# Merging two branches of a decoder layer: transfers issued by ScalarE at fixed units instead of by SP

## The chip, the cores and the metric

The kernel runs on one core of one Trainium2 chip. The metric is the device time of one execution in microseconds (us). Before the change three runs took 2646.43, 2651.6 and 2653.45 us; the median is 2651.6. Profiles are taken by the hardware on one further execution each.

The engines are TensorE (PE, matrix products), VectorE (DVE), ScalarE (ACT), GpSimd (POOL) and SyncE (SP). Each has its own in-order instruction stream. A transfer (DMA) is started by an instruction in the stream of one of them; an instruction that has to wait for a semaphore holds up everything behind it in its stream, transfers included.

## The reference

One hybrid decoder layer in float32, batch 1, sequence 1024, width 1024: half a SwiGLU FFN, a token mixer with two branches on one normalised input, half a second SwiGLU FFN, a final RMSNorm. Branch A is a gated DeltaNet; branch B attention over the top 256 causal keys per query, chosen by an indexer. Cut to the part in question:

```python
o_sa = dsa_attention(cq, ckv, k_idx, w_idx, w_uq, w_uk, w_uv, w_iq, rel_bias)   # branch B
o_dn = rmsnorm(o_dn, dn_out_norm) * silu(dn_z)                                 # branch A
merged = sigmoid(gate_a) * o_dn + sigmoid(gate_b) * o_sa
x = x + merged @ w_o
# inside dsa_attention, per block of 128 queries and head (8 heads of 128):
p = softmax(where(valid, q_lat @ c_sel * 128**-0.5 + bias, -inf))
o = (p @ c_sel) @ w_uv
```

## The kernel before, in words

Products keep float32 accuracy by splitting each operand into a high part and a remainder. `split` (L109) casts the high part on ScalarE (L111) and subtracts on VectorE or POOL (L112); `mm3` (L137) then issues three matmuls, high·high (L139), high·remainder (L140) and remainder·high (L141).

The stage in question is the attention (`attn_head`, L1295), some 1600 to 1900 us into the execution. All is laid out transposed: 128 channels of a head on the partitions, 1024 positions along the row. The heads 0 to 7 follow each other. A head has four units g in the order 0, 1, 3, 2; unit g holds the query blocks 2g and 2g+1, against all keys up to them, so units 3 and 2 are the long ones. In a unit

- TensorE makes the logits `pl`; VectorE adds bias and mask and keeps the row maximum (`a_mx`, L1322); ScalarE takes the exponential with the row's sum (`a_sum`, L1327);
- TensorE transposes the probabilities into `pp` (L1335); ScalarE casts `ph` (L1338), VectorE subtracts `plo` (L1339); TensorE accumulates `pao` = probabilities times values;
- ScalarE copies `pao` to `osa` (L1344). This copy ends the unit.

Work for later heads runs between: `attn_qk` (queries and keys of the next head: products `pqk`, ScalarE's p at L1288, VectorE's p at L1289), asked for after unit 1 with a priority that lets it move forward, and `attn_values` once per pair of heads, before the even one (products `pav`, then `vh` L1271 and `vl` L1272). Their weights w_uq, w_uk and w_uv come by SP into a rotating buffer `w_raw` (`attn_weights`, L1253) and are split on ScalarE and POOL into `wa`.

The merge (L1359) is done twice per head, for the first 512 positions (h = 0) after unit 1 and for the others (h = 1) after unit 2. Branch A (`odd`), its gate (`zgd`) and tanh of half the gate of branch B (`gbd`) lie in DRAM; a half of a head of each is 128 x 512, 256 KB. The softmax's denominators stand one per partition (128 x 4) and are wanted along the row: `a_rd` writes 0.5 / sum as 512 single numbers to DRAM (L1378), and `a_rb` reads them back to all partitions (L1380). SP issues `od`, `zg`, `gb` (L1369), `a_rd` and `a_rb` in a row, each with one buffer but `a_rd`. One or two units later `done` (L1382) runs: POOL `od` *= `zg` (L1383), VectorE `osa` *= `a_rb` (L1384) and `osa` = (`gb` + 1) `osa` (L1385), POOL `mr` = `od` + `osa` (L1386). The last half uses TensorE to spread the denominators instead of `a_rd` and `a_rb`.

The order of each engine's instructions is set when the program is built, by a scheduler that simulates the engines with priorities; `issue_after` keeps an instruction behind another one in it, and `high_priority` moves one forward. So an edit moves instructions of other parts too.

Of the kernel before, what the change touches and what calls it, by code (L numbers as in the profile page):

```python
# [20 lines left out]
P = 128  # L21
# [49 lines left out]
class Layer:  # L71
# [1188 lines left out]
    def attn_values(self, pair, p, ps):  # L1260
        nc = self.nc
        wh, wl = self.attn_weights(self.I["w_uv"][0][:, 2 * pair:2 * pair + 2, :].rearrange("r h d -> r (h d)"), 256, p, "wuv")
        vh = p.tile([P, NT, 256], F32R, name="vh", tag="vh", bufs=1)
        vl = p.tile([P, NT, 256], F32R, name="vl", tag="vl", bufs=1)
        for t in range(0, NT, 2):
# [5 lines left out]
            nc.scalar.copy(vh[:, t:t + 2, :], pv)  # L1271
            nc.vector.tensor_sub(vl[:, t:t + 2, :], pv, vh[:, t:t + 2, :])  # L1272
# [22 lines left out]
    def attn_head(self, hd, p, ps, qk, values, merged, ahead):  # L1295
# [6 lines left out]
        osa = p.tile([P, S], F32, name="osa", tag="osa", bufs=2)  # L1302
        for g in (0, 1, 3, 2):
            probs = []
# [25 lines left out]
            for j in range(0, 2 * g + 2, 2):  # L1330
# [9 lines left out]
                for i in range(2):  # L1340
                    a, b = (0, 256) if i == 0 else (256, n)
                    out = po[:, 0:256] if b - a == 256 else po[:, 128:256]
                    self.mm3(out, vh[:, j + i, hv], vl[:, j + i, hv], ph[:, a:b], pl_[:, a:b], j + i == 0, j + i == 2 * g + 1)
            nc.scalar.copy(osa[:, ts(g, 256)], po[:, 0:256])  # L1344
            if g == 1:
                ahead()
            for late in self.outs:
                late[0] -= 1
            while self.outs and self.outs[0][0] == 0:
                with self.tc.issue_after(dve.ins):  # L1350
                    self.outs.pop(0)[1]()
            if g in (1, 2):
                out = self.merge(hd, g // 2, sums, osa, p, ps, merged)
                if hd == H - 1 and g == 2:
                    out()
                else:
                    self.outs.append([g, out])

    def merge(self, hd, h, sums, osa, p, ps, merged):  # L1359
# [6 lines left out]
        od, zg, gb = (p.tile([P, 512], F32, name=n, tag=n, bufs=1) for n in ("od", "zg", "gb"))  # L1366
        v = ts(h, 512)
        for x, src in ((od, self.odd[hd][:, v]), (zg, self.zgd[hd][:, v]), (gb, self.gbd[hd][:, v])):
            nc.sync.dma_start(x, src)  # L1369
        if hd == H - 1 and h == 1:  # L1370
# [5 lines left out]
        else:  # L1376
            rd = self.dram.tile([512], F32, name="a_rd", tag="a_rd", bufs=2)
            nc.sync.dma_start(rd.rearrange("(t i) -> i t", i=P), r)  # L1378
            rb = p.tile([P, 512], F32, name="a_rb", tag="a_rb", bufs=1)
            nc.sync.dma_start(rb, rd.partition_broadcast(P))  # L1380

        def done():  # L1382
# [302 lines left out]
```

## Time and profile before

| | |
|---|---|
| median of three runs | 2651.6 us |
| the profiled execution | 2654.08 us |
| its span on the profile | 2652.1 us |
| mean granted TensorE clock | 0.971 |
| busy: TensorE, VectorE, ScalarE, POOL | 2519.1, 1737.9, 1198.3, 970.9 us |

The span is what the trace covers; the execution's own time is 2.0 us longer. Busy times are sums over the span. The granted clock is a share of TensorE's full 2.4 GHz; in a stretch at 0.5 the engine ran at 1.2 GHz. Waits are listed by the instruction that waits and the one it waited for.

### The profile page before, as it was taken

To read this page: it belongs to the slowest core of one execution; us is meant where nothing else is said; L and a number is where in the kernel's file an instruction comes from. 1 tells how busy PE (TensorE), PEld (TensorE's weight loads), DVE (VectorE), ACT (ScalarE), POOL (GpSimd) and SP (SyncE) were. 2 spreads that over 40 slices of the span, in tenths; PEclk is the share of its full clock that TensorE was granted. 3 is DMA by queue.
4 is the path that set the end of the run, shared out by engine and by line. 5 is a ranking of instruction groups with operands and counts; after the bars stand their busy time and mean duration, and the time that the engine had idled before them with its cause. 6 is when DMAs were issued, how large, how long until landed. Compare 5 with 4: busy or idle time off the path is not lost.

```text
span 2652.1 us, 36132 instructions
## 1 busy us (share of the span) xinstructions
PE 2519.1 (95%) x12526; PEld 2054.9 (77%) x12526; DVE 1737.9 (66%) x3424; ACT 1198.3 (45%) x2338; POOL 970.9 (37%) x748
## 2 busy tenths in 40 slices
PE   6999999999999899989999999779898999999998
PEld 5788888888787688777778778678776888888886
DVE  7655555676555677999566866566668555546676
ACT  6444344333434665544368446445434434434333
POOL 5555444343434233332100002333446545543340
PEclk8999999999999899999999999889998999999999
DMA  5443346753444155445633323333632344347642
GB/s 168 136 143 129 113 146 219 255 194 101 120 114 122 41 140 139 115 124 123 200 124 116 124 82 74 82 76 78 200 111 94 102 143 143 127 150 263 224 151 75
DMA packets 375607, 356.67 MB, mean 134 GB/s; under 512 B 95417, under 2 KB 279553, under 8 KB 374401
## 3 DMA queue, kind: packets, MB, share of 16 engines
q1 hardware_dynamic: 371840, 348.60, 42.1%
q10 hardware_dynamic: 2304, 4.20, 0.4%
q0 software_dynamic: 1280, 1.57, 0.3%
q8 instruction: 99, 1.62, 0.3%
q14 instruction: 84, 0.68, 0.1%
HBM read 238.28 MB, written 116.01 MB: 134 GB/s over the span
## 4 chain that ended last, share of the span: by engine, by line
PE 40%; DVE 9%; DMA 6%; issue 2%; ACT 1%; POOL 1%; SPq 0%; DVEq 0%; POOLq 0%; ACTq 0%
PE pst L139 7%; PE pst L141 7%; PE pst L140 7%; PE pin L141 2%; PE pin L139 2%; PE pin L140 2%; DVE sb_p L1034 2%; DMA a_rd<-a_r 2%; DMA od<-odd 1%; PE pn L1221 1%; PE po L1230 1%; PE pv L1216 1%; DVE cv_y L923 1%; PE pq L1211 1%; PE pwo L141 1%
## 5 line engine op out<-in xcount | busy, mean ns | idle before, releaser
L140 PE MATMUL pst<-p,w_hi 128*128 128x512 f32 x992 | 392.1, 395 | 8.6 <-DVE p L112 8.5
L139 PE MATMUL pst<-p,w_hi 128*128 128x512 f32 x992 | 393.2, 397 | 4.1 <-ACT p L111 2.3
L141 PE MATMUL pst<-p,w_hi 128*128 128x512 f32 x992 | 391.3, 395 | 0.5 <-DVE w_hi L112 0.5
L139 PE MATMUL pin<-p,w_hi 128*128 128x512 f32 (+1 forms) x848 | 342.1, 405 | 6.0 <-DVE cv_y L923 4.2
L111 ACT CAST w_hi<-w_raw 128x512 fp32r<-128x512 f32 (+3 forms) x294 | 204.1, 695 | 311.7 <-PE pst L141 135.8
L140 PE MATMUL pin<-p,w_hi 128*128 128x512 f32 (+1 forms) x848 | 340.5, 402 | 0.5 <-DVE p L112 0.5
L141 PE MATMUL pin<-p,w_lo 128*128 128x512 f32 (+1 forms) x848 | 340.8, 402 | 0.0
L112 DVE TENSOR_TENSOR w_lo<-w_raw,w_lo 128x512 fp32r<-128x512 f32 (+1 forms) x196 | 188.3, 963 | 167.2 <-ACT w_lo L111 165.6
L140 PE MATMUL pst<-p,w_lo 128*128 128x512 f32 x744 | 292.7, 394 | 3.7 <-DVE p L112 3.7
L141 PE MATMUL pst<-p,w_lo 128*128 128x512 f32 x744 | 292.2, 393 | 1.2 <-DVE w_lo L112 1.2
L139 PE MATMUL pst<-p,w_lo 128*128 128x512 f32 x744 | 290.6, 396 | 0.5 <-ACT c L360 0.5
L140 PEld LDWEIGHTS pst<-p,w_hi 128*128 128x128 f32 x992 | 188.3, 190 | 53.9 <-DVE p L112 12.9
L139 PEld LDWEIGHTS pst<-p,w_hi 128*128 128x128 f32 x992 | 188.8, 190 | 47.3 <-ACT p L111 3.5
L141 PEld LDWEIGHTS pst<-p,w_hi 128*128 128x128 f32 x992 | 188.5, 190 | 43.0 <-DVE w_hi L112 1.3
L111 ACT CAST w_lo<-w_raw 128x512 fp32r<-128x512 f32 (+1 forms) x200 | 115.7, 582 | 207.4 <-PE pst L141 97.8
L139 PEld LDWEIGHTS pin<-p,w_hi 128*128 128x128 f32 (+1 forms) x848 | 161.6, 191 | 42.7 <-DVE cv_y L923 4.5
L141 PEld LDWEIGHTS pin<-p,w_lo 128*128 128x128 f32 (+1 forms) x848 | 161.5, 190 | 37.7 <-issue 3.8
L140 PEld LDWEIGHTS pin<-p,w_hi 128*128 128x128 f32 (+1 forms) x848 | 161.6, 191 | 37.5 <-issue 4.0
L373 DVE TENSOR_TENSOR c<-c,pst 128x512 f32<-128x512 f32 x132 | 89.9, 682 | 150.9 <-PE pst L141 118.1
L112 POOL TENSOR_TENSOR w_lo<-w_raw,w_hi 128x1024 fp32r<-128x1024 f32 (+1 forms) x43 | 107.0, 2488 | 199.4 <-ACT w_hi L111 189.4
L140 PEld LDWEIGHTS pst<-p,w_lo 128*128 128x128 f32 x744 | 140.7, 189 | 35.1 <-DVE p L112 4.9
L141 PEld LDWEIGHTS pst<-p,w_lo 128*128 128x128 f32 x744 | 140.7, 189 | 33.5 <-DVE w_lo L112 2.1
(427 smaller groups left out, 5393.8 us busy)
## 6 DMA issues: line engine op xcount, KB each, us to landing
p<-mixd SPq DMA_DIRECT2D x144, 256.0 KB, 5.4
w_raw<-in_w_in_dram SPq DMA_DIRECT2D x52, 512.0 KB, 4.1
w_raw<-in_ffn_wg_dram SPq DMA_DIRECT2D x44, 512.0 KB, 3.6
w_raw<-in_ffn_wu_dram SPq DMA_DIRECT2D x44, 512.0 KB, 4.0
mixd<-t_hi SPq DMA_DIRECT2D x72, 256.0 KB, 4.3
mixd<-t SPq DMA_DIRECT2D x72, 256.0 KB, 3.8
w_raw<-in_ffn_wd_dram SPq DMA_DIRECT2D x48, 384.0 KB, 4.1
actd<-c SPq DMA_DIRECT2D x70, 256.0 KB, 2.0
```

The costliest lines, as they stand in the source:

```text
L111: self.nc.scalar.copy(hi, raw)
L112: self.pin((self.nc.vector if engine == "vector" else self.nc.gpsimd).tensor_sub(lo, raw, hi))
L139: mm(ps, lhsT=wh, rhs=rh, start=first, stop=False, **kw)
L140: mm(ps, lhsT=wh, rhs=rl, start=False, stop=False, **kw)
L141: mm(ps, lhsT=wl, rhs=rh, start=False, stop=last, **kw)
L373: nc.vector.tensor_add(c[i, h], c[i, h], bank["y" if m == 1 else "z"])
L923: nc.vector.scalar_tensor_tensor(y[:, n:512], pps[h][:, 0:512 - n], cw[:, j:j + 1], y[:, n:512], ALU.mult, ALU.add)
L1034: nc.vector.tensor_mul(v, T[:, 0:i, 0:i].rearrange("p j c -> p c j"), L[:, None, 0:i, i].to_broadcast([P, i, i]))
L1211: nc.tensor.matmul(pq[:, i, :], lhsT=kq[:, h, ts(c, P)], rhs=old[:, h, :], start=True, stop=True)
L1216: nc.tensor.matmul(pv[r, i, :], lhsT=X[r, h, :], rhs=vb[r, h, :], start=True, stop=True)
L1221: nc.tensor.matmul(pn[:, i, :], lhsT=kd[r, h, :], rhs=vn[r, h, :], start=True, stop=True)
L1230: nc.tensor.matmul(po[r, i, :], lhsT=at[r, h, :], rhs=vn[r, h, :], start=True, stop=True)
```

## The change

All transfers of the merge are issued by ScalarE, right behind the copy that ends a unit: after unit 1 the `a_rb` and `gb` of the previous head's second half, this head's first `a_rd`, and the second half of `zg`; after unit 3 the `a_rb` and `gb` of the first half; after unit 2 the second `a_rd`, and for the next head `odd` and the first half of `zg`. `odd` is loaded for a whole head at once (128 x 1024) into the tile `mr` in which the merged head ends up, and multiplied there by POOL (`other_branch`, L1389 of the changed kernel) in units 0 and 3; `od` is gone. The products with `a_rb` and `gb` on VectorE follow one unit after `a_rb`. `merge` and `other_branch` are generators that advance from unit to unit. `osa` becomes three tiles of 512 columns, `zg` keeps one buffer, `a_rb` and `gb` get two. `vh` and `vl` become four tiles each, of two key blocks. Lines of the changed kernel: `a_rd` L1376, `a_rb` L1381, `gb` L1383, `odd` L1392, `zg` L1396, POOL's product L1398, its sum L1387.

SP's queue in front of the weights of the third pair of heads (`w_uv`; `w_uq` and `w_uk` are those of queries and keys, `near` a bias tile), before:
```order
L1369 DMA zg<-zgd 128x512
L1380 DMA a_rb<-a_rd 128x512
L1369 DMA gb<-gbd 128x512
L1369 DMA od<-odd 128x512
L1378 DMA a_rd<-a_r 128x4x1
L1369 DMA zg<-zgd 128x512
L1256 DMA w_raw<-in_w_uv_dram 128x2x256
L1380 DMA a_rb<-a_rd 128x512
L1369 DMA gb<-gbd 128x512
L1256 DMA w_raw<-in_w_uq_dram 128x2x128
```

and now, in front of the same pair's w_uv (the last row but one):
```order
L1256 DMA w_raw<-in_w_uk_dram 128x2x128
L584 DMA near<-nb_wide 128x256
L1256 DMA w_raw<-in_w_uv_dram 128x2x256
L1256 DMA w_raw<-in_w_uq_dram 128x2x128
L1256 DMA w_raw<-in_w_uk_dram 128x2x128
L1256 DMA w_raw<-in_w_uq_dram 128x2x128
L584 DMA near<-nb_wide 128x256
L1256 DMA w_raw<-in_w_uk_dram 128x2x128
L584 DMA near<-nb_wide 128x256
L1256 DMA w_raw<-in_w_uv_dram 128x2x256
L1256 DMA w_raw<-in_w_uq_dram 128x2x128
```

Before, the load of w_uv stands behind four loads of the merge, an `a_rd` and an `a_rb`. Now SP holds weights and `near` only.

ScalarE from the copy that ends unit 1 of head 1 to the one that ends unit 3, before:
```order
L1344 COPY osa<-pao 128x256
L1327 ACTIVATE w_hi,a_sum<-w_hi,a_nm 128x640
L1338 CAST ph<-pp 128x512
L1327 ACTIVATE w_lo,a_sum<-w_lo,a_nm 128x768
L1327 ACTIVATE w_hi,a_sum<-w_hi,a_nm 128x128
L1327 ACTIVATE w_lo,a_sum<-w_lo,a_nm 128x256
L1338 CAST ph<-pp 128x384
L1327 ACTIVATE w_hi,a_sum<-w_hi,a_nm 128x384
L1338 CAST ph<-pp 128x512
L1327 ACTIVATE w_lo,a_sum<-w_lo,a_nm 128x512
L1344 COPY osa<-pao 128x256
```

and now (the last rows follow the copy of unit 3):
```order
L1344 COPY osa<-pao 128x256
L1381 DMA a_rb<-a_rd 128x512
L1383 DMA gb<-gbd 128x512
L1376 DMA a_rd<-a_r 128x4x1
L1396 DMA zg<-zgd 128x512
L1338 CAST ph<-pp 128x512
L1338 CAST ph<-pp 128x384
L1338 CAST ph<-pp 128x512
L1344 COPY osa<-pao 128x256
L1381 DMA a_rb<-a_rd 128x512
```

Before, casts and exponentials alone stand between the copies. Now four transfers stand there, the first of them (`a_rb`) needing a landed `a_rd`, and behind the copy of unit 3 comes an `a_rb` that needs the `a_rd` issued behind the copy of unit 1. The exponentials of the next head's first units have moved ahead of the first copy.

POOL within head 2 (`mr_14141` is head 2's merged tile; `wa` of 256 columns in both halves belongs to w_uq or w_uk, of 512 to w_uv; `nb` a bias), before:
```order
L112 TENSOR_TENSOR wa<-w_raw,wa 128x256
L112 TENSOR_TENSOR wa<-w_raw,wa 128x512
L1386 TENSOR_TENSOR mr_14141<-od,osa 128x512
L112 TENSOR_TENSOR wa<-w_raw,wa 128x256
L1383 TENSOR_TENSOR od<-od,zg 128x512
L1309 TENSOR_TENSOR nb<-near,mask_5848 128x256
```

and now:
```order
L112 TENSOR_TENSOR wa<-w_raw,wa 128x256
L1398 TENSOR_TENSOR mr_14141<-mr_14141,zg 128x512
L112 TENSOR_TENSOR wa<-w_raw,wa 128x256
L112 TENSOR_TENSOR wa<-w_raw,wa 128x512
L1309 TENSOR_TENSOR nb<-near,mask_5848 128x256
L1309 TENSOR_TENSOR nb<-near,mask_5849 128x256
L1309 TENSOR_TENSOR nb<-near,mask_5846 128x256
L112 TENSOR_TENSOR wa<-w_raw,wa 128x256
```

Before, the product `od` *= `zg` follows the splits of `wa` in this stretch; now the product on the merged tile stands between them, in front of the second small one.

```diff
--- before.py
+++ after.py
@@ -1260,16 +1260,15 @@
     def attn_values(self, pair, p, ps):
         nc = self.nc
         wh, wl = self.attn_weights(self.I["w_uv"][0][:, 2 * pair:2 * pair + 2, :].rearrange("r h d -> r (h d)"), 256, p, "wuv")
-        vh = p.tile([P, NT, 256], F32R, name="vh", tag="vh", bufs=1)
-        vl = p.tile([P, NT, 256], F32R, name="vl", tag="vl", bufs=1)
+        vh, vl = ([p.tile([P, 2, 256], F32R, name=n, tag=f"{n}{t}", bufs=1) for t in range(NT // 2)] for n in ("vh", "vl"))
         for t in range(0, NT, 2):
             pv = ps.tile([P, 2, 256], F32, name="pav", tag="qk")
             for i in range(2):
                 for k in range(2):
                     lh, ll = (x[2 + k][t // 4][:, ts((t + i) % 4, P)] for x in self.lat)
                     self.mm3(pv[:, i, :], lh, ll, wh[:, k, :], wl[:, k, :], k == 0, k == 1)
-            nc.scalar.copy(vh[:, t:t + 2, :], pv)
-            nc.vector.tensor_sub(vl[:, t:t + 2, :], pv, vh[:, t:t + 2, :])
+            nc.scalar.copy(vh[t // 2], pv)
+            nc.vector.tensor_sub(vl[t // 2], pv, vh[t // 2])
         return vh, vl
 
     def attn_qk(self, hd, p, ps):
@@ -1292,15 +1291,16 @@
             qk.append((hi, lo))
         return qk
 
-    def attn_head(self, hd, p, ps, qk, values, merged, ahead):
+    def attn_head(self, hd, p, ps, qk, values, merged, ahead, other):
         nc = self.nc
         near = self.near_tile(p, hd)
         (qh, ql), (kh, kl) = qk
         vh, vl = values
         hv = slice((hd % 2) * P, (hd % 2) * P + P)
         sums = self.stat.tile([P, NT], F32, name="a_sum")
-        osa = p.tile([P, S], F32, name="osa", tag="osa", bufs=2)
         for g in (0, 1, 3, 2):
+            if g in (0, 3):
+                osa = p.tile([P, 512], F32, name="osa", tag="osa", bufs=3)
             probs = []
             for b in (2 * g, 2 * g + 1):
                 W = (b + 1) * P
@@ -1340,21 +1340,21 @@
                 for i in range(2):
                     a, b = (0, 256) if i == 0 else (256, n)
                     out = po[:, 0:256] if b - a == 256 else po[:, 128:256]
-                    self.mm3(out, vh[:, j + i, hv], vl[:, j + i, hv], ph[:, a:b], pl_[:, a:b], j + i == 0, j + i == 2 * g + 1)
-            nc.scalar.copy(osa[:, ts(g, 256)], po[:, 0:256])
-            if g == 1:
-                ahead()
-            for late in self.outs:
-                late[0] -= 1
-            while self.outs and self.outs[0][0] == 0:
-                with self.tc.issue_after(dve.ins):
-                    self.outs.pop(0)[1]()
-            if g in (1, 2):
-                out = self.merge(hd, g // 2, sums, osa, p, ps, merged)
-                if hd == H - 1 and g == 2:
-                    out()
-                else:
-                    self.outs.append([g, out])
+                    self.mm3(out, vh[j // 2][:, i, hv], vl[j // 2][:, i, hv], ph[:, a:b], pl_[:, a:b], j + i == 0, j + i == 2 * g + 1)
+            act = nc.scalar.copy(osa[:, ts(g % 2, 256)], po[:, 0:256])
+            ahead(hd, g)
+            with self.tc.issue_after(dve.ins), self.tc.issue_after(act.ins):
+                for out in self.outs:
+                    next(out, None)
+                if g in (1, 2):
+                    out = self.merge(hd, g // 2, sums, osa, p, ps, merged)
+                    next(out)
+                    self.outs = self.outs[-1:] + [out]
+                other(hd, g)
+            if hd == H - 1 and g == 2:
+                for out in self.outs:
+                    for _ in out:
+                        pass
 
     def merge(self, hd, h, sums, osa, p, ps, merged):
 
@@ -1363,11 +1363,9 @@
         r = self.stat.tile([P, 4], F32, name="a_r")
         nc.vector.reciprocal(r, sums[:, ts(h, 4)])
         nc.vector.tensor_scalar_mul(r, r, 0.5)
-        od, zg, gb = (p.tile([P, 512], F32, name=n, tag=n, bufs=1) for n in ("od", "zg", "gb"))
         v = ts(h, 512)
-        for x, src in ((od, self.odd[hd][:, v]), (zg, self.zgd[hd][:, v]), (gb, self.gbd[hd][:, v])):
-            nc.sync.dma_start(x, src)
-        if hd == H - 1 and h == 1:
+        last = hd == H - 1 and h == 1
+        if last:
             rb = ps.tile([P, 512], F32, name="a_rp", tag="pt")
             for t in range(4):
                 d = p.tile([P, P], F32, name="a_d", tag="near", bufs=2)
@@ -1375,17 +1373,30 @@
                 nc.tensor.matmul(rb[:, ts(t, P)], lhsT=self.ones, rhs=d, start=True, stop=True)
         else:
             rd = self.dram.tile([512], F32, name="a_rd", tag="a_rd", bufs=2)
-            nc.sync.dma_start(rd.rearrange("(t i) -> i t", i=P), r)
-            rb = p.tile([P, 512], F32, name="a_rb", tag="a_rb", bufs=1)
-            nc.sync.dma_start(rb, rd.partition_broadcast(P))
-
-        def done():
-            nc.gpsimd.tensor_mul(od, od, zg)
-            nc.vector.tensor_mul(osa[:, v], osa[:, v], rb)
-            nc.vector.scalar_tensor_tensor(osa[:, v], gb, 1.0, osa[:, v], ALU.add, ALU.mult)
-            nc.gpsimd.tensor_add(merged[:, v], od, osa[:, v])
-
-        return done
+            nc.scalar.dma_start(rd.rearrange("(t i) -> i t", i=P), r)
+            yield
+            if h == 1:
+                yield
+            rb = p.tile([P, 512], F32, name="a_rb", tag="a_rb", bufs=2)
+            nc.scalar.dma_start(rb, rd.partition_broadcast(P))
+        gb = p.tile([P, 512], F32, name="gb", tag="gb", bufs=2)
+        nc.scalar.dma_start(gb, self.gbd[hd][:, v])
+        yield
+        nc.vector.tensor_mul(osa, osa, rb)
+        nc.vector.scalar_tensor_tensor(osa, gb, 1.0, osa, ALU.add, ALU.mult)
+        (nc.vector if last else nc.gpsimd).tensor_add(merged[:, v], merged[:, v], osa)
+
+    def other_branch(self, hd, p, merged):
+
+        nc = self.nc
+        nc.scalar.dma_start(merged, self.odd[hd])
+        for h in range(2):
+            v = ts(h, 512)
+            zg = p.tile([P, 512], F32, name="zg", tag="zg", bufs=1)
+            nc.scalar.dma_start(zg, self.zgd[hd][:, v])
+            yield
+            nc.gpsimd.tensor_mul(merged[:, v], merged[:, v], zg)
+            yield
 
 
     def out_proj(self, m, ps, after_tile, after_half):
@@ -1617,15 +1628,23 @@
                 raw = [mlp.tile([P, S], F32, name=f"mr{k}", tag=f"mr{k}") for k in range(NK)]
                 qk = self.qk
 
-                def ahead():
-                    if len(qk) < H:
+                others = [self.other_branch(k, p, raw[k]) for k in range(H)]
+                next(others[0])
+
+                def other(hd, g):
+                    for k, at in ((hd, (0, 1, 3)), (hd + 1, (2,))):
+                        if k < H and g in at:
+                            next(others[k], None)
+
+                def ahead(hd, g):
+                    if hd + 1 < H and g == 1:
                         with self.tc.high_priority(offset=AHEAD):
-                            qk.append(self.attn_qk(len(qk), (p, "wqk", 2), ps))
+                            qk.append(self.attn_qk(hd + 1, (p, "wqk", 2), ps))
 
                 for i in range(H):
                     if i % 2 == 0:
                         vals = self.attn_values(i // 2, p, ps)
-                    self.attn_head(i, p, ps, qk[i], vals, raw[i], ahead)
+                    self.attn_head(i, p, ps, qk[i], vals, raw[i], ahead, other)
                 hs.close()
                 mp = self.pool(ms, "merged", 1, "right")
                 hi, lo = ([mp.tile([P, S], F32R, name=f"{n}{k}", tag=f"{n}{k}") for k in range(NK)] for n in ("mh", "ml"))
```

## Rows read from the trace of the kernel before

**Rows 1.** Three stretches: busy us and count of each engine, PEclk, DMA share, GB/s
```profile
1700.00:1720.00 20.00, 9.11 (x30) 7.13 (x31) 6.03 (x18) 5.02 (x13) 5.72 (x6) 0.57 0.37 90
1720.00:1740.00 20.00, 20.00 (x137) 18.30 (x136) 15.00 (x54) 11.80 (x29) 9.34 (x13) 1.00 0.15 34
1625.50:1894.50 269.00, 224.57 (x1398) 198.56 (x1398) 171.94 (x503) 133.43 (x303) 96.34 (x104) 0.90 0.34 81
```

**Rows 2.** ScalarE's timeline, each head's last copy: start, us, engine, line, [wait]
```profile
1654.09 0.37 ACT L1344 COPY osa<-pao 128x256 f32<-128x256 f32 x1 [0.34 <-PE pao L141]
1681.14 0.39 ACT L1344 COPY osa<-pao 128x256 f32<-128x256 f32 x1
1727.05 0.36 ACT L1344 COPY osa<-pao 128x256 f32<-128x256 f32 x1
1751.23 0.39 ACT L1344 COPY osa<-pao 128x256 f32<-128x256 f32 x1
1797.70 0.36 ACT L1344 COPY osa<-pao 128x256 f32<-128x256 f32 x1
1822.04 0.39 ACT L1344 COPY osa<-pao 128x256 f32<-128x256 f32 x1
```

**Rows 3.** TensorE's waits, 1600 to 1905: us in total, times, longest
```profile
PE pqk L139 <- DVE p L1289: 22.2, 4, 9.1
PE pl L139 <- DVE a_mx L1322: 9.9, 3, 5.1
PE pqk L141 <- POOL wa L112: 1.7, 2, 1.0
```

**Rows 4.** TensorE's timeline, three first products of `pqk`
```profile
1701.77 0.79 PE L139 MATMUL pqk<-p,wa 128*128 128x512 f32 x1 [2.90 <-DVE p L1289]
1715.04 0.79 PE L139 MATMUL pqk<-p,wa 128*128 128x512 f32 x1 [8.15 <-DVE p L1289]
1784.90 0.80 PE L139 MATMUL pqk<-p,wa 128*128 128x512 f32 x1 [9.10 <-DVE p L1289]
```

**Rows 5.** ScalarE's waits, 1600 to 1905
```profile
ACT wa L111 <- DMA w_raw<-in_w_uv_dram: 36.5, 3, 17.7
```

**Rows 6.** Waits in SP's queue, 1600 to 1905
```profile
SPq L1369 <- POOL od L1383: 91.0, 15, 12.5
SPq L1380 <- DMA a_rd<-a_r: 85.2, 12, 11.2
```

**Rows 7.** DMA issues: of 1600 to 1900, and of the page; KB each, us to landing
```profile
a_rd<-a_r SPq DMA_DIRECT2D x15, 2.0 KB, 11.5
actd<-c SPq DMA_DIRECT2D x70, 256.0 KB, 2.0
```

**Rows 8.** Transfers in the chain of waits, 1590 to 1910; last line: SP's timeline
```profile
1683.33 10.89 DMA od<-odd
1703.94 9.19 DMA w_raw<-in_w_uv_dram
1727.77 11.67 DMA a_rd<-a_r
1753.47 10.99 DMA a_rd<-a_r
...
1682.62 0.42 SPq L1378 DMA_DIRECT2D a_rd<-a_r  x1
```

**Rows 9.** VectorE's waits, 1600 to 1905
```profile
DVE osa L1384 <- DMA a_rb<-a_rd: 26.7, 9, 6.3
```

**Rows 10.** ScalarE's timeline, one DMA issue
```profile
1591.04 0.33 ACTq L1125 DMA_DIRECT2D gbd<-tb  x1
```

**Rows 11.** Costliest groups by form, 1590 to 1910: busy, mean ns | idle before
```profile
L1338 ACT CAST ph<-pp 128x512 fp32r<-128x512 f32 x48 | 28.1, 587 | 18.1 <-PE pp L1335 16.2 <-PE pao L141 1.4
L1383 POOL TENSOR_TENSOR od<-od,zg 128x512 f32<-128x512 f32 x16 | 22.3, 1395 | 112.4 <-DMA od<-odd 62.3 <-issue 50.1
L112 POOL TENSOR_TENSOR wa<-w_raw,wa 128x256 fp32r<-128x256 f32 x14 | 10.7, 767 | 28.4 <-ACT wa L111 28.4
```

## The prediction

> **What bounds the kernel now.** I began with busy time by stretch. From the first to the last copy of an attention result (the stage that the change touches) TensorE is busy 224.57 of 269.0 us [rows 1]: 44.4 us are idle, and the granted clock averages 0.90. The reader is to see that no other engine comes near: VectorE has 171.9 and ScalarE 133.4 us of work there. So TensorE's own work sets the end, plus whatever makes it wait.
>
> The losses are uneven. Window 1700 to 1720 has TensorE busy for 9.11 us at a clock of 0.57; the next 20 us are full, 137 matmuls at clock 1.00, so 0.146 us each [rows 1]. The ends of five heads stand at 1681.14, 1727.05, 1751.23, 1797.70 and 1822.04, with head 0's at 1654.09 [rows 2]: head 1 takes 27.05 us, head 2 45.91, head 3 24.18, head 4 46.47, head 5 24.34. The even heads carry `attn_values` besides, but that is not all.
>
> The waits name the rest. TensorE waits 22.2 us in four waits for VectorE's p (L1289) before `pqk`, 1.7 us for POOL's `wa` there, and 9.9 us in three for `a_mx` before `pl` [rows 3]. Two of the four stand in head 2 (2.90 and 8.15) and the longest, 9.10, in head 4 [rows 4]. VectorE is not the cause: behind it ScalarE stands 36.5 us in three waits for the weights w_uv [rows 5]. ScalarE works in order, so the `pqk` results queue behind the cast of w_uv, and VectorE's halves of them with it. And w_uv is late because SP's queue stands in order too: 85.2 us until an `a_rd` has landed (L1380), 91.0 us until POOL has freed `od` (L1369) [rows 6]. `a_rd` is 2 KB in 512 pieces of four bytes, and takes a median of 11.5 us to land [rows 7]; the chain of waits has it at 10.99 and 11.67, an `od` issued right behind one (1682.62, then 1683.33) at 10.89, and w_uv at 9.19 [rows 8].
>
> **The change part by part.** I sum against the profiled execution, 2654.08 us (span 2652.1), 2.5 us above the median of 2651.6.
>
> *Removed: the weight stall.* SP keeps only weights and `near`, so w_uv is issued as soon as its buffer is free. The waits before `pqk` go: 22.2 + 1.7 = 23.9 us [rows 3]. In 1700 to 1720 a mean of 0.57 means 17.2 us at the lower level (1.2 GHz); TensorE was busy for at most 9.1 us of them, and half of that is what the clock cost, some 4.0 a head [rows 1]. Heads 2 and 4 together: 92.38 - 23.9 - 8.0 = 60.5, so 30.2 us each undisturbed. If the clock stays low, 8 us less is gained.
>
> The rows show besides that what follows an `a_rd` into SP's queue is slow: `od` 10.89, w_uv 9.19 us [rows 8]. A rule of the Trainium skill ("DMA: Bandwidth & Descriptors", section "Queues, rings and completion order") speaks against this part of the change: the increment that tells of a landed transfer comes only after all earlier writes of the same DMA engine, whatever queue they came by. By it w_uv from SP would still land with an `a_rd` of ScalarE's, up to some 10 us late; by the rows, which show it within one queue only, w_uv is free of it. I take the gain whole, because w_uv is now issued early enough to bear 10 us, and keep the other as rival C.
>
> *Removed: VectorE's wait for `a_rb`.* 26.7 us in nine [rows 9]; what TensorE sees of it is at most the 9.9 us of `a_mx` [rows 3], and 5.1 of these stand in head 1.
>
> *Added: the same waits on ScalarE.* Some seventy transfers at 0.33 us of issue [rows 10] are 23 us of ScalarE's 135 idle ones; by themselves nothing, at most a few times 1 us between a copy and a cast. What counts is that ScalarE now stops at each `a_rb` (L1381) until the `a_rd` one or two units earlier has landed. Queued behind it are the casts `ph`, the next exp and the next copy of `osa`; TensorE waits for all three. Between a copy and the next TensorE has, by the order, 56, 46 and 49 matmuls in odd heads (their means; 8.2, 6.7 and 7.2 us at 0.146) and 62, 81 and 61 in head 2. An `a_rd` at 11.0 us [rows 8] is therefore covered in even heads from unit 1 to unit 3 (11.8 us) and not elsewhere.
>
> The price of `a_rd` in its new queue stands in no row. Below it is bounded by the 2.0 us of `actd`, 256 KB in large pieces [rows 7], above by its waits behind loads, 11.67 [rows 8]; I take 11.0, since its own rows all lie there and it keeps its 512 pieces. An odd head is then a chain on ScalarE: copy and issue 0.7, `a_rd` 11.0, three issues 1.0, the next `a_rd` 11.0, two issues 0.66, one `ph` 0.59 [rows 11], and of the 49 matmuls to the last copy (7.2 us) what TensorE could not do beforehand, about 4.7: together 29.65, with 1.35 for the clock after the idle stretches (a third of the 4.0 above) 31.0. Three of them: 93.0 against 27.05 + 24.18 + 24.34 = 75.57, so +17.4. Bounds: the waits fully covered leave about 24.2 a head (-3), `a_rd` at 11.67 and the clock's full 4.0 give 35 (+29).
>
> *Heads 2 and 4.* The `a_rb` at unit 1 finds 62 matmuls, 9.05 us, before it against 0.35 + 11.0: +2.3. Then POOL: the product of the second half (L1398) now stands before the two-column casts `wa` (L112) that feed `pqk`, and it waits for a `zg` that ScalarE issues last, behind the next `a_rd`. Issued some 14 us after the head's start, landed at 25, product 1.40, cast 0.77 [rows 11]: 27 to 29.5, where TensorE wants it at about 24, so 4.3 us, and 3.0 for the clock. Bounds: 0, if `zg` lands like other loads, and 9.1, the longest of the waits now [rows 4]. 30.2 + 2.3 + 4.3 + 3.0 = 39.8; two of them 79.6 against 92.4: -12.8.
>
> *The rest.* Head 0 has the same POOL order (+4.5), head 6 has no weights and comes out even, head 7 loses an `a_mx` wait (-2), the merge of the last head ends later because its `gb` is issued after the last copy (+2), and the first `od` waits on ScalarE for the stores of the branch before it (+1): +5.5, bounds -5 (half of the 9.9) and +12. Cost nothing: the split of `vh` and `vl` (same instructions), and the addition that moves to VectorE once at the end (under 1 us).
>
> Sum: +17.4 - 12.8 + 5.5 = +10.1, or 2664.2; less 2.5 for the median, **2662 us**.
>
> **The rivals.** *A, the waits stay covered (faster).* The place is the `a_rb` on ScalarE. If `a_rd` lands in 7.1 us, which is what SP waits for it on average (85.2 / 12) [rows 6], every chain is shorter than TensorE's own work: heads 2 and 4 give the whole -31.9, head 1 -3, the rest -2 to 0: 2617. By my sum each us of `a_rd` is worth eight (two in each of three odd heads, one in each of two even), so it decides at 11.0 - 10.1 / 8 = 9.7 us. For it: only the one queue stood behind it before, and the low SP wait. Against it: 10.99, 11.67 and a median of 11.5.
>
> *B, the clock.* Short repeated idleness keeps TensorE at 1.2 GHz, 4.0 us in each of the eight heads instead of the 1.35 to 3.0 counted: about +15, and `a_rd` at 11.67 adds 5: 2682. For it: 0.57 with half the time idle [rows 1]; against it: no wait I forecast is as long as 8 us.
>
> *C, the weights still stand behind `a_rd`.* If the 9.19 to 10.89 us of [rows 8] come back across the two queues and w_uv isn't early enough, about half of the 23.9 is not gained: 2674. For it: w_uv's own buffer must first be freed by the casts before it, so it can't be issued at will. Against it: both of SP's long waits [rows 6] are gone from in front of it.
>
> *D, nothing moves*: ScalarE's new waits and the old ones cancel: 2651.
>
> **How the numbers follow.** This kernel's measurement can tell about 0.3%, 8 us, from no change. Forecast 0.43, own range 2647 to 2677; A 0.30; B 0.11; C 0.10; D 0.06. Faster is A and a sliver of the forecast: 0.31. Same, 2644 to 2660, is D and two fifths of the forecast: 0.23. Slower: 0.46. The range runs from 2624, leaving about half of A out, to 2684, leaving a third of B out.
>
> **What would show it.** Right: ScalarE's waits list L1381 behind `a_rd` with some 60 to 90 us and w_uv with none; `pqk` waits in heads 2 and 4 for `wa` instead of p; odd heads of 29 to 32 us; `a_rd` still at 10 to 12. Wrong: `a_rd` under 9.7 us (then A), odd heads near 24, or w_uv still in the list (C). A stretch from first to last copy of under 269 us would overturn the forecast.

## The result, and the profile after

The changed kernel took 2686.77 us (median of four runs, 2681.82 to 2695.97) against 2652.52 for the kernel before beside it: a ratio of 1.0138, 95% interval 1.0105 to 1.0171. It is slower by 34 us; the forecast was +10, and its range ended 3 us below the measured time.

From the first to the last copy of `osa`, and then from the last copy of head 6 to that of head 7, and from there to the last broadcast `n_rb` of the norm that follows the output projection, the changed kernel's windows read (busy us and count of each engine, PEclk, DMA share, GB/s):

```profile
1632.20:1922.20 290.00, 226.33 (x1370) 200.19 (x1368) 157.71 (x495) 131.64 (x300) 90.57 (x102) 0.89 0.34 71
1872.30:1921.80 49.50, 28.40 (x145) 23.69 (x144) 21.13 (x49) 19.94 (x39) 11.47 (x8) 0.79 0.25 64
1921.80:2025.40 103.60, 97.88 (x446) 80.02 (x444) 58.17 (x87) 34.95 (x50) 38.52 (x26) 0.98 0.53 170
```

The first row answers the last of [rows 1]: 290.0 us instead of 269.0, TensorE idle for 63.7 instead of 44.4. For the two others the kernel before has:

```profile
1852.20:1894.10 41.90, 33.62 (x179) 27.85 (x178) 30.36 (x59) 22.58 (x43) 19.51 (x15) 0.92 0.42 118
1894.10:1984.80 90.70, 89.97 (x418) 74.22 (x417) 53.07 (x76) 32.27 (x47) 37.33 (x25) 1.00 0.55 181
```

Nearly the same matmuls (591 recorded now, 597 before) take 153.1 us instead of 132.6 in the last two windows together. The last copies of heads 0 to 5, which answer [rows 2]:

```profile
1663.98 0.35 ACT L1344 COPY osa<-pao 128x256 f32<-128x256 f32 x1
1693.37 0.38 ACT L1344 COPY osa<-pao 128x256 f32<-128x256 f32 x1
1733.85 0.37 ACT L1344 COPY osa<-pao 128x256 f32<-128x256 f32 x1 [0.24 <-PE pao L141]
1769.15 0.38 ACT L1344 COPY osa<-pao 128x256 f32<-128x256 f32 x1
1811.60 0.37 ACT L1344 COPY osa<-pao 128x256 f32<-128x256 f32 x1 [2.57 <-PE pao L141]
1842.05 0.38 ACT L1344 COPY osa<-pao 128x256 f32<-128x256 f32 x1
```

From such rows, the first `pav` and the last `n_rb`, the stage divides as follows (us; "end" runs from the last copy of head 7 to the last `n_rb`; the last two rows are of the repeats h1 and h2 below):

| kernel | to first copy | head 0 | 1 | 2 | 3 | 4 | 5 | 6 | 7 | end | sum |
|---|---|---|---|---|---|---|---|---|---|---|---|
| before | 14.1 | 28.5 | 27.0 | 45.9 | 24.2 | 46.5 | 24.3 | 30.2 | 41.9 | 90.6 | 373.3 |
| after | 14.5 | 31.7 | 29.4 | 40.5 | 35.3 | 42.4 | 30.5 | 30.2 | 49.5 | 103.6 | 407.5 |
| before, again | 14.3 | 28.5 | 19.6 | 42.8 | 24.4 | 37.4 | 24.5 | 25.4 | 41.6 | 90.3 | 348.9 |
| after, again | 13.2 | 30.7 | 27.7 | 39.9 | 28.7 | 42.7 | 28.3 | 31.8 | 42.4 | 104.5 | 390.0 |

The stage alone differs by 34.2 us, as much as the medians do. (The profiled execution of the changed kernel, 2695.97 us, is its longest; its first `pav` is 6.3 us later, at 1617.8. Two further executions, g1 and h2 below, have it at 1611.8 and 1612.0, so that part is scatter.)

TensorE's waits, 1600 to 1950 (us in total, times, longest), answer [rows 3]:

```profile
PE pao L139 <- ACT ph L1338: 33.8, 6, 10.3
PE pqk L141 <- POOL wa L112: 11.0, 3, 6.2
PE pwo L140 <- POOL ml L112: 9.2, 1, 9.2
PE pl L139 <- DVE a_mx L1322: 4.3, 4, 3.3
```

Here `pwo` are the products of the output projection; their operands `mh` and `ml` are the high part (cast on ScalarE) and the remainder (subtracted on VectorE, for three of the eight heads on POOL) of the merged heads. The waits for p behind w_uv are gone, and so is w_uv from ScalarE's waits [rows 5], though w_uq now stands there with 18.6 us in three. In their place TensorE waits for ScalarE's casts and for POOL. ScalarE's timeline in head 3 (start, us) shows why:

```profile
1733.86 0.38 ACTq L1376 DMA_DIRECT2D a_rd<-a_r  x1
...
1745.97 0.33 ACTq L1381 DMA_DIRECT2D a_rb<-a_rd  x1
...
1746.82 0.45 ACTq L1376 DMA_DIRECT2D a_rd<-a_r  x1
1750.86 0.33 ACTq L1396 DMA_DIRECT2D zg<-zgd  x1
1760.07 0.33 ACTq L1381 DMA_DIRECT2D a_rb<-a_rd  x1
```

12.1 and 13.3 us lie between each `a_rd` and its `a_rb`: two landings in series, 25.4 of the head's 35.3 us. ScalarE stops at `zg` too, 3.6 us between the second `a_rd` and `zg` (5.4 and 3.4 in heads 1 and 5): `zg` has one buffer, and POOL's product frees it only after the `zg` before has landed. ScalarE's waits before `ph`, 1600 to 1950, name both:

```profile
ACT ph L1338 <- POOL mr L1398: 17.2, 2, 8.7
ACT ph L1338 <- DMA a_rd<-a_r: 15.1, 3, 9.4
```

POOL's largest wait, and the landings (KB, median us; the last row is `zg` of the kernel before):

```profile
POOL mr L1398 <- DMA zg<-zgd: 127.9, 13, 16.5
```
```profile
zg<-zgd ACTq DMA_DIRECT2D x16, 256.0 KB, 10.0
...
a_rd<-a_r ACTq DMA_DIRECT2D x15, 2.0 KB, 11.6
...
zg<-zgd SPq DMA_DIRECT2D x16, 256.0 KB, 3.8
```

`a_rd` lands as it did in SP's queue [rows 7], and `zg`, 3.8 us before the change, now takes 10.0: issued behind an `a_rd`, it lands 0.2 to 3.7 us behind it in the four cases for which the trace has both. In head 7 TensorE's timeline has both waits one after the other:

```profile
1889.73 0.58 PE L139 MATMUL pao<-ph,vh 128*128 128x256 f32 x1 [10.27 <-ACT ph L1338]
1904.17 0.80 PE L140 MATMUL pwo<-ml,w_hi 128*128 128x512 f32 x1 [9.15 <-POOL ml L112]
```

### The profile page after: what moved, and what is told of

Its sections match the earlier page's. It is cut to its first block, busy times and chain, and to the rows that moved or that the text cites. A ratio compares the mean times of both kernels' runs of the same rounds, so it can differ in the third digit from the quotient of the medians.

```text
span 2694.3 us, 36064 instructions
## 1 busy us (share of the span) xinstructions
PE 2530.2 (94%) x12526; PEld 2062.7 (77%) x12526; DVE 1736.6 (64%) x3425; ACT 1199.7 (45%) x2338; POOL 966.4 (36%) x747
## 4 chain that ended last, share of the span: by engine, by line
PE 39%; DVE 8%; DMA 6%; issue 3%; ACT 2%; POOL 1%; ACTq 0%; SPq 0%; DVEq 0%; POOLq 0%
PE pst L139 6%; PE pst L141 6%; PE pst L140 6%; PE pin L141 2%; PE pin L140 2%; PE pin L139 2%; DMA a_rd<-a_r 2%; DVE sb_p L1034 2%; PE po L1230 1%; PE pn L1221 1%; PE pv L1216 1%; DVE cv_y L923 1%; PE pq L1211 1%; DMA zg<-zgd 1%; DVE p L112 1%
## 5 line engine op out<-in xcount | busy, mean ns | idle before, releaser
L112 DVE TENSOR_TENSOR w_lo<-w_raw,w_lo 128x512 fp32r<-128x512 f32 (+1 forms) x196 | 193.8, 991 | 168.9 <-ACT w_lo L111 167.1
```

What stands on the lines that cost most here:

```text
L112: self.pin((self.nc.vector if engine == "vector" else self.nc.gpsimd).tensor_sub(lo, raw, hi))
```

## The experiments

Theory: what costs is the landing of `a_rd`, on ScalarE at `a_rb` and on POOL at the `zg` that lands with it. Rival: the queue or the places cost, whatever is waited for. Ratios are to the kernel before on the chip of the set, with their intervals; there it took 2633 to 2642 us.

**The same places, issued by SP** (e1).

```diff
-            nc.scalar.dma_start(...)   # in merge and other_branch
+            nc.sync.dma_start(...)
```

> The changed kernel with every transfer of the merge at the same places in the program, but issued by SP. Theory (the 10 to 13 us landing of a_rd is what is waited for, on ScalarE at the a_rb and on POOL at the zg that lands with it): ScalarE is free again, so the waits of TensorE for ph (33.8 us) go, but POOL's and SP's stay and the weights stand behind an a_rd again: 2650 to 2675 us. Rival (the places and the order cost the time, whoever issues): still 2680 to 2692 us, with TensorE waiting for ph as before.

1.0147 (1.0122 to 1.0172): not the fall that the theory asked for, so its number was a miss. But the waits are others. SP's and ScalarE's first rows, 1600 to 1950, and TensorE's for `ph`:

```profile
SPq L1381 <- DMA a_rd<-a_r: 145.0, 15, 11.4
```
```profile
ACT wa L111 <- DMA w_raw<-in_w_uv_dram: 47.4, 3, 24.5
```
```profile
PE pao L139 <- ACT ph L1338: 19.6, 3, 19.0
```

SP stands 145 us for `a_rd` instead of 85 [rows 6], and w_uv is later than ever. The waits for `ph` do not go, as the theory had it; they fall from 33.8 to 19.6 us, and 19.0 of them are one wait behind a w_uv that SP issued at 1733.47, after standing for an `a_rd` until 1733.06. Either queue pays; the run alone doesn't part theory and rival.

**`a_rd` in four pieces** (e2).

```diff
-            nc.scalar.dma_start(rd.rearrange("(t i) -> i t", i=P), r)
+            rt = ps.tile([P, 512], F32, name="a_rt", tag="pt")
+            nc.tensor.transpose(rt[0:4, 0:P], r, self.ident)
+            rs = p.tile([4, P], F32, name="a_rs", tag="a_rs", bufs=1)
+            nc.vector.tensor_copy(rs, rt[0:4, 0:P])
+            nc.scalar.dma_start(rd.rearrange("(t i) -> t i", i=P), rs)
```

> The changed kernel with one thing altered: TensorE transposes the 128 x 4 denominators, and a_rd writes them as 4 rows of 512 bytes instead of 512 single numbers. Theory: a_rd lands in 2 to 4 us instead of 11.6, the a_rb, gb and zg beside it too, so the stops of ScalarE and POOL go: 2605 to 2635 us, faster than both. Rival (ScalarE's queue and the order cost the time, not the landing): a_rd may land sooner but the time stays at 2675 to 2690 us.

0.9937 (0.9915 to 0.9959): faster than both kernels, by one edit. TensorE from the first `pav` to the last `n_rb`, and its longest wait:

```profile
1611.70:1959.00 347.30, 327.42 (x1912) 282.86 (x1911) 228.81 (x632) 177.70 (x367) 138.24 (x140) 0.97 0.37 115
```
```profile
PE pao L139 <- ACT ph L1338: 5.1, 5, 1.5
```

19.9 us idle instead of 69.4 (407.6 less 338.2 busy). The waits for `wa` and `ml` are gone too, so POOL's came from the same landing. This decides for the theory: places and queue are those of the changed kernel, and the loss is gone.

**No `a_rd` at all** (e3): each half as the last one, on TensorE.

```diff
-        if last:
+        gb = ...; nc.scalar.dma_start(gb, self.gbd[hd][:, v]); yield
+        if True:
             rb = ps.tile([P, 512], F32, name="a_rp", tag="pt")
```

> The changed kernel with no a_rd and no a_rb at all: every half spreads its denominators with four small products on TensorE, as only the last half did. Theory: all waits for a_rd go; 60 more matmuls at some 0.11 to 0.28 us and 60 multiplications on VectorE cost 7 to 15 us of it: 2610 to 2645 us. Rival (ScalarE's queue and the order cost the time): od, gb and zg still leave from ScalarE, so 2675 to 2700 us.

1.0016 (1.0001 to 1.0030), 2646.2 us and just above the expected range: the waits for `ph` fall to 8.2 us and those for `wa` and `ml` go, but 60 more products (0.275 us for each of their two passes) on the engine that sets the end, with VectorE's multiplications between, give back what e2 has over the kernel before.

**`a_rb` one unit later** (e4; in short, `self.outs` keeps one more entry besides).

```diff
             yield
+            yield
             if h == 1:
```

> The changed kernel with each a_rb (and its gb and the products after it) one unit later, so that 13 us or more lie between an a_rd and its a_rb; a_rd is as slow as before. Theory: TensorE's waits for ph (33.8 us) shrink below 12, POOL's zg still lands with the a_rd, so its waits (pqk for wa 11.0, pwo for ml 9.2) stay: 2655 to 2672 us. If ScalarE's stop were not what costs: 2680 to 2692 us.

1.0077 (1.0050 to 1.0103), as expected in time. TensorE's waits, and w_uv's landing:

```profile
PE pl L139 <- DVE a_mx L1322: 14.7, 10, 6.0
PE pqk L139 <- DVE p L1288: 13.5, 2, 7.9
PE pwo L140 <- POOL ml L112: 5.9, 1, 5.9
PE pao L139 <- ACT ph L1338: 3.9, 3, 2.2
```
```profile
w_raw<-in_w_uv_dram SPq DMA_DIRECT2D x3, 256.0 KB, 9.1
```

The waits for `ph` fall from 33.8 to 3.9 us. Those for `a_mx` grow from 4.3 to 14.7; the expectation had no place for them. New is that w_uv, from SP, takes 9.1 us beside an `a_rd` from ScalarE, and p is late again: rival C's mechanism, across the two queues.

**The old places with `a_rd` in four pieces** (f1): the same edit in the kernel before, on SP.

> The kernel before, with only the transposed a_rd of the second experiment (4 rows of 512 bytes); all transfers stay on SP at their old places. Theory (the landing of a_rd is the whole cost, in either queue): SP's waits for a_rd and the late w_uv go, and the time comes down as far as with the change, ratio 0.988 to 0.996 to the kernel before. Rival (the new places bring part of that gain themselves): 0.996 to 1.002.

0.9887 (0.9870 to 0.9904), the fastest of its set and 0.5% better than e2, each against the kernel before beside it. The stage, and SP's wait for `a_rd` from 1600 to 1905:

```profile
1610.00:1936.00 326.00, 316.95 (x1911) 277.97 (x1911) 236.92 (x631) 177.46 (x367) 145.07 (x141) 0.99 0.38 122
```
```profile
SPq L1384 <- DMA a_rd<-a_rs: 16.5, 15, 3.0
```

9.05 us idle; SP stands for `a_rd` 1.1 us each time on average, instead of 7.1 [rows 6]. So with the landing gone the rest of the change brings no gain; it costs some 13 us. Of these TensorE's waits for `ph` show 4.5 (5.1 in e2, 0.6 here); that they come from the issues, which stand between a copy and the next cast, is argued. Heads 1, 3 and 5 take 77.5 us in e2 and 64.4 here; the cause of the rest is not shown. `ml` on VectorE besides (g3):

> The kernel before with the transposed a_rd, and ml all on VectorE. Its TensorE waits 4.1 us for ml on POOL before the output projection; if VectorE is free there, 2 to 6 us under the kernel with the transposed a_rd alone, ratio 0.986 to 0.988. If VectorE, busier than POOL, hands ml over later: the same or slower, 0.989 to 0.992.

0.9880 (0.9855 to 0.9906), no difference that can be told from f1.

**`zg` from SP** (f3).

```diff
-            nc.scalar.dma_start(zg, self.zgd[hd][:, v])
+            nc.sync.dma_start(zg, self.zgd[hd][:, v])
```

> The changed kernel with one thing altered: zg is issued by SP, all else by ScalarE. If a transfer from SP's queue is not held up by an a_rd of ScalarE's queue, zg lands in some 4 us, POOL's waits for zg fall from 128 us to below 60, and pqk for wa and pwo for ml (20.2 us) go: 10 to 20 us under the changed kernel, ratio 1.006 to 1.010. If it is (rival C's rule), zg still lands after 8 to 12 us beside an a_rd and the time stays within 6 us: 1.011 to 1.016.

1.0109 (1.0089 to 1.0130), between the two cases in time, so the landings have to tell. Those of 1858 to 1863, where an `a_rd` was issued at 1858.53 by ScalarE and a `zg` at 1862.09 by SP:

```profile
zg<-zgd SPq DMA_DIRECT2D x1, 256.0 KB, 7.1
a_rd<-a_r ACTq DMA_DIRECT2D x1, 2.0 KB, 10.4
```

1862.1 + 7.1 and 1858.5 + 10.4 both end at 1869: the later transfer of the other queue landed with the `a_rd`. It is no single case: of five `zg` that SP issued while an `a_rd` of ScalarE was under way, and for which the trace has both landings, each landed 0.2 to 3.6 us behind that `a_rd` and took 7.1 to 11.3 us; three that SP issued with no `a_rd` under way took 2.6 to 2.7. Over the stage `zg` takes a median of 7.4 us and w_uv 10.4.

**The end: single edits.** The loss of 20.6 us in head 7 and behind it was not in the sum. First `ml` on VectorE (f2), then the last two pairs of `a_rd` and `a_rb` on TensorE (f4), then both (g2), and the changed kernel again for comparison (g1), with `vh` and `vl` whole again (g4). The diff is in short; f4 and g2 also issue `gb` a unit earlier there and give `a_d` a buffer of its own.

```diff
-   self.split(..., "gpsimd" if k % 3 == 1 else "vector")      # f2, g2
+   self.split(..., "vector")
-   if last:                                                   # f4, g2
+   if last or hd * 2 + h in (2 * H - 3, 2 * H - 2):
-   vh, vl = ([p.tile([P, 2, 256], ...) ...] ...)              # g4
+   vh, vl = (p.tile([P, NT, 256], ...) ...)
```

> The changed kernel with one thing altered: the remainders ml of the merged heads (three of eight heads, before the output projection) are all subtracted on VectorE instead of in part on POOL, where they queue behind the product that waits for zg. Theory (head 7 and the end lose 20 us, of which 9.2 is TensorE's wait for ml and some 4 to 5 the low clock after it): 8 to 14 us under the changed kernel, ratio 1.008 to 1.011. Rival (ScalarE's stop in head 7, 10.3 us, and its clock are the whole): within 4 us of the changed kernel, 1.012 to 1.016.

> The changed kernel with the last two pairs of a_rd and a_rb (head 6's second half, head 7's first) replaced by TensorE's spreading, as the last half has it; the other thirteen stay. Theory (20.6 us are lost in head 7 and behind it because of these two landings): that stretch comes back to within 5 us of the kernel before, 14 to 20 us under the changed kernel, ratio 1.006 to 1.009, the heads before unchanged. Rival (the end is late for another reason, the weights of the output projection or the order there): 0 to 6 us, 1.012 to 1.015.

> The changed kernel with both edits at its end: ml on VectorE, and the last two pairs of a_rd and a_rb replaced by TensorE's spreading. Theory (POOL's ml behind zg, and ScalarE's stop at a_rb, are the two causes of head 7's loss): the single edits gave about 14 and 10 us, together 16 to 24 us under the changed kernel, and head 7 with the end within 4 us of the kernel before. Rival (both edits take away the same wait, and the end is late for a third reason): no better than the single ones, 10 to 15 us under the changed kernel.

> The changed kernel itself once more, beside the other three of this set. If what it loses is eight times the landing of a_rd, as the sum of the prediction had it, it loses less where a_rd lands sooner: the experiments so far show 9.5 to 10.5 us instead of 11.6, so 8 to 16 us less than the 34 of the first comparison, ratio 1.007 to 1.012. If the loss doesn't hang on the landing: 1.0138 again, at least 1.012.

> The changed kernel with vh and vl as one tile each again, the part of the change that the prediction priced at nothing. If that holds: within 6 us of the changed kernel. If the split lets the values of the next pair of heads be made earlier, this kernel is 6 to 15 us slower than the changed one, with TensorE or ScalarE waiting at vh (L1270).

f2 1.0084 (1.0065 to 1.0104), f4 1.0099 (1.0079 to 1.0120), g2 1.0105 (1.0077 to 1.0133), g1 1.0113 (1.0088 to 1.0138), g4 1.0095 (1.0066 to 1.0125). f2 met its number, but against g1 only 8 us are left of it, with intervals that overlap; f4 and g2 fell short. In both the waits for `ph` and `ml` at the end are gone but for 0.2 us, and others stand there: in f4 6.2 us for VectorE's remainder of the projection's weights (1.6 in h2, the changed kernel) and 3.5 for the operands of the spreading. That the spreading brings the first is argued. g4: the split of `vh` and `vl` costs or brings nothing that can be measured.

**The end: where the landings count.** Both kernels with a profile on one chip (h1, h2), and four pieces in heads 6 and 7 only (h3), or in heads 0 to 5 only (h4).

```diff
+            if hd >= H - 2:        # h3; h4: hd < H - 2
+                ...                # the transposed a_rd of e2
+            else:
                 nc.scalar.dma_start(rd.rearrange("(t i) -> i t", i=P), r)
```

> The kernel before once more, with a profile on the chip of this set, whose a_rd lands sooner than in the first comparison. Theory (the kernel before pays for the landing too, in SP's queue): its a_rd lands in 9.5 to 10.5 us instead of 11.5 and the stage from the first pav to the last n_rb takes 350 to 362 us instead of 373. Rival (before and after differ in what they pay): 370 to 376 us.

> The changed kernel beside it on the same chip, for a comparison by heads: stage 380 to 384 us; against the kernel before the odd heads +3 to +7 us each, heads 2 and 4 -4 to 0, head 7 and the end together +10 to +16.

> The changed kernel with a_rd as 4 rows of 512 bytes in heads 6 and 7 only (three of the fifteen). Theory (head 7 and the end lose their time to these landings): heads 6, 7 and the end come to where they stand with all fifteen in rows (25.7 and 134.6 us, against 29.4 and 144.8), so 10 to 16 us under the changed kernel, ratio 1.005 to 1.0085, with heads 0 to 5 as in the changed kernel. Rival (the end loses to something else): 0 to 6 us, 1.009 to 1.0125.

> The complement: a_rd as 4 rows in heads 0 to 5, single numbers in heads 6 and 7. Theory: heads 0 to 5 come to 29.5, 24.3, 32.8, 27.8, 32.8 and 25.4 us, some 20 to 25 us less than in the changed kernel, and the end stays: ratio 1.000 to 1.004. If the two parts do not add up to the gain of all fifteen (46 us at 0.9937 against 1.0113), a delay in one part is made up or passed on in the other.

h1 1.0008 (0.9986 to 1.0029), h2 1.0106 (1.0065 to 1.0148), h3 1.0056 (1.0035 to 1.0076), h4 0.9969 (0.9952 to 0.9987). The landing differs from the first comparison, and the kernel before pays for it as well: 9.0 us and a stage of 348.9 in h1, against 11.5 and 373.3. The table above has h2's misses: the stage takes 390.0 us where 380 to 384 were expected; head 7 with the end loses 15.0, as expected, but head 4, expected to gain or stay, loses 5.3, and head 6, even the first time, 6.4. Heads 6, 7 and the end take 178.7 us in h2 and 160.7 in h3; the medians of the two, 2663.15 and 2651.58, are 11.6 us apart, and their runs don't overlap. So the last three landings are a cause of the loss there. Unexpectedly these heads take 160.7 in h4 as well, where the last three `a_rd` are single numbers as before (the trace has no landing for them), and h4 came out faster than its expectation of 1.000 to 1.004: the loss goes when either the last three or the twelve before them are short. ScalarE's order suggests why. In the changed kernel, from the copy of unit 1 of head 7 (13 casts `mh`, 42 products of the output projection behind them):

```
L1344 COPY osa<-pao 128x256
L1381 DMA a_rb<-a_rd 128x512
...
L1338 CAST ph<-pp 128x512 x2
L1327 ACTIVATE w_hi,a_sum<-w_hi,a_nm 128x640
L111 CAST mh_17318<-mr_14139 128x512
```

In h4 eleven `mh` stand ahead of that copy, the last rows being:

```
L111 CAST mh_17369<-mr_14142 128x512
L1344 COPY osa<-pao 128x256
L1388 DMA a_rb<-a_rd 128x512
```

The work that could fill TensorE stands behind the stop in the one and ahead of it in the other. So I moved the stop (i1: this one `a_rb` a unit later; in short, `self.outs` keeps one more entry besides), and then `ml` to VectorE besides (i2):

```diff
+            if hd == H - 2 and h == 1:
+                yield
             rb = p.tile([P, 512], F32, name="a_rb", tag="a_rb", bufs=2)
```

> The changed kernel with one a_rb (and its gb) moved: that of head 6's second half goes one unit later, behind the copy of unit 3 of head 7, so that the casts mh of the merged heads, which feed the first 42 products of the output projection, stand in front of ScalarE's stop and not behind it. a_rd is as slow as before. Theory (the end loses because that filling work is queued behind the stop): heads 0 to 6 as in the changed kernel, head 7 with the end 5 to 11 us shorter than 146.9, ratio 1.006 to 1.0085. Rival (POOL's ml behind zg is what holds the output projection): 0 to 3 us, 1.0095 to 1.012.

> The same, and ml on VectorE besides, so that neither half of the split merged heads waits for a landing. Theory: head 7 with the end at 134 to 138 us, 9 to 13 us shorter than in the changed kernel, ratio 1.0055 to 1.008. If only one of the two queues counts, the same as the kernel with the moved a_rb alone, within 3 us.

i1 1.0112 (1.0095 to 1.0130): no gain, against the theory and as its rival, POOL's `ml`, had it. i2 1.0078 (1.0058 to 1.0098), 9 us better than i1 on the same chip, with no overlap of their runs. TensorE's waits, 1850 to 1990, in the changed kernel (h2), with `ml` moved (f2), with the stop moved (i1) and with both (i2):

```profile
PE pao L139 <- ACT ph L1338: 11.4, 2, 7.8
PE pwo L140 <- POOL ml L112: 5.7, 1, 5.7
```
```profile
PE pao L139 <- ACT ph L1338: 8.8, 2, 8.6
```
```profile
PE pwo L140 <- POOL ml L112: 7.9, 1, 7.9
PE pao L139 <- ACT ph L1338: 5.3, 2, 3.0
```
```profile
PE pao L139 <- ACT ph L1338: 1.9, 1, 1.9
```

Head 7 with the end: 146.9, 141.3, 144.6 and 132.5 us; the kernel before has 131.9 (h1). By these profiles two stops look as if they stood in series, ScalarE's for `a_rb` and POOL's for `zg`: without the first the second is longer (5.7 becomes 7.9), and only without both is head 7 with the end as short as before. But the four profiled executions lie 8.2 us above, 0.5 below, 4.4 above and 8.2 below the medians of their kernels, and the medians do not follow: f2 (1.0084), with `ml` alone moved, can't be told from i2 (1.0078). So what is shown is that `ml` behind POOL's wait for `zg` costs the end some 9 us. That ScalarE's stop in head 7 costs anything besides is not shown.

## Why the prediction was wrong

The sign was right, and the mechanism in heads 0 to 6 in the main; the size was not: +10.1 was forecast, the stage lost 34.2.

- *The weight stall goes.* Right in kind: p and w_uv are gone from the waits. Heads 2 and 4 gained 5.4 and 4.1 us, 9.5 together against 12.8. In the repeat, where the kernel before loses less to the landing, head 2 gained 2.9 and head 4 lost 5.3.
- *Odd heads as a chain of two landings on ScalarE.* Right: 31.0 each forecast; 29.4, 35.3 and 30.5 measured, +19.6 over the three against +17.4. Where `a_rd` lands in 9.9 us (h2) they are 27.7, 28.7 and 28.3, as the chain would have it. Two things differ from it: the stop at `zg`, 3.4 to 5.4 us in each of the three, was priced as an issue of a third of a us, and ScalarE's list has no L1381 with 60 to 90 us but 46.9 us before `ph`, by `zg`'s buffer, `a_rd` and "issue".
- *POOL's product ahead of `wa`.* Right for heads 2 and 4, 3.9 and 6.2 us (4.3 each). Head 0 lost 3.2 (4.5 forecast), but only 0.9 of it is this wait: TensorE is busy for 30.7 us there instead of 28.5, with 198 products instead of 185. That number came by luck.
- *Head 6 even.* So it was, 30.2 before and after, but not in the repeat, 25.4 and 31.8.
- *The failing step is the one under "The rest": "head 7 loses an `a_mx` wait (-2), the merge of the last head ends later ... (+2)".* It gave 0 for head 7 and the end; they lost 20.6, nearly the whole miss of 24. I had priced ScalarE's stop for odd heads and left it out in head 7, and had seen POOL's product ahead of `wa` and not that it stands ahead of `ml` as well. In head 7 no later head's work lies behind the wait: the filler is the output projection, and it needs ScalarE's `mh` and POOL's `ml`, both queued behind a landing. The profile has 10.27 and 9.15 us for the two, and a granted clock of 0.79 instead of 0.92 over the head. The runs show the landings of heads 6 and 7 as a cause (h3, 11.6 us), together with the earlier ones (h4), and `ml` behind `zg` as a way by which they cost (i2 against i1, 9.4 us); ScalarE's part is argued from the waits alone, for i1 gained nothing. What makes up the rest of the 20.6 stays open.
- *Rival A* (faster) asked for an `a_rd` under 9.7 us. It didn't come: 11.6. The figure was wrong besides: with 9.5 to 9.9 us (g1, h2) the change still loses 1.1%, because the kernel before gains from a faster landing too (h1). I had let the landing vary on one side of the comparison only.
- *Rival B* didn't come as put: from the first to the last copy the granted clock averages 0.89 against 0.90. It rose in heads 2 and 4 (0.81 and 0.82, now 0.92 each) and fell in heads 3 and 5 (1.00 each, now 0.85 and 0.83) and in head 7. Its sum is off besides: 4.0 us in eight heads less the 10.1 counted in five are 22, not 15.
- *Rival C.* Its mechanism is real, though the changed kernel escapes it: there w_uv is issued in time and lands in a median of 4.3 us. In e4 and f3 it doesn't: 9.1 and 10.4. The Trainium skill ("DMA: Bandwidth & Descriptors", section "Queues, rings and completion order") has it as a rule that an increment waits for all earlier writes of that DMA engine, whatever their queue. f3 agrees with it: there `zg` from SP landed with the `a_rd` of ScalarE at 1869. The rule doesn't tell all: in the changed kernel a `zg` issued 1.5 us ahead of an `a_rd` (1872.67, 1874.13), with no other under way, took 10.5 us too.
- The split of `vh` and `vl` at nothing: right (g4).

## What to carry to other kernels

When a transfer is waited for in an in-order queue, look at why it lands late before moving the wait to another queue: here moving it cost 1.1 to 1.4%, and writing the same 2 KB in 4 pieces instead of 512 gained 1.1% on the kernel before. When the sum of a repeated stage is made, do its last round by itself, with the work that fills it there and every queue that this work passes. Where two stops stand behind one cause, take each away alone and both together, and compare medians: one profile each put ScalarE's stop beside POOL's here, and the medians did not.

## What was not expected of the hardware

A landing of 2 KB depended on its pieces far more than on its bytes: medians of 9.0 to 11.6 us with 512 of four bytes, whichever queue; with 4 of 512 bytes SP waits for it 1.1 us on average and 3.0 at most (f1; the trace gives no landing of its own for that form). Number and size of the pieces changed together, so neither is shown alone. The Trainium skill ("DMA: Bandwidth & Descriptors", "Specifications") puts the size for line rate at 512 bytes and more. No run here tells where between 4 and 512 bytes the cost falls. And the landing of the same transfer in the same program differed between the comparisons: medians of 11.5 (before) and 11.6 us (after) in the first, 9.0 and 9.9 in h1 and h2, with 19 us between the medians of the kernel before. Whether the chip makes that difference is open: on one chip the kernel before had medians of 2641.75 (set e) and 2634.82 us (set h).
